# Feed-forward of a two-layer streaming encoder: the first three chunks' partial sums go into x by a ScalarE copy and an accumulating DMA

## The chip, the core and the metric

The kernel runs on one core of a Trainium2 chip. The engines named here are PE (TensorE, matrix products), DVE (VectorE), ACT (ScalarE), POOL (GpSimd) and SP (SyncE, which issues most loads); each serves its own queue strictly in order, and waits for other engines and for transfers by semaphores. TensorE writes its results into banks of PSUM; DVE and ACT read them there. The metric is the device time of one execution in microseconds (us), lower is better; a profiled execution also gives a span, from its first to its last instruction of the program.

## What is computed

A trunk of two layers over 512 tokens of width 1024, batch 1, in float32. Cut to what matters:

```python
def conv_ffn(xn, w_up, conv_w, conv_b, w_down):
    h = causal_depthwise_conv(xn @ w_up, conv_w) + conv_b
    g, u = jnp.split(h, 2, axis=-1)
    return (jax.nn.gelu(g) * u) @ w_down

for layer in range(2):
    x = x + mixer(rms_norm(x, mix_norm[layer]))
    x = x + memory_cross_attention(rms_norm(x, xattn_norm[layer]), ...)
    x = x + conv_ffn(rms_norm(x, ffn_norm[layer]), ...)
return rms_norm(x, final_norm)
```

The mixer is attention of two kinds in layer 0 and a gated recurrence (mLSTM) in layer 1. The feed-forward is the place of the change: the inner width is 2816, so `w_up` is 1024 x 5632 (a gate half and a value half) and `w_down` is 2816 x 1024.

## The kernel before

**Layout.** x is held transposed in SBUF for the whole run: eight tiles `x[m]` of 128 features x 512 tokens, float32. Every product is made of float32r operands split into a high and a low part, and `mm3` (lines 282 to 286) issues three matmuls for each: high x high, high x low, low x high. Weights come as blocks of 128 x 1024 (or 128 x 512) by SP into a raw tile (`raw`, `dr`, `sa`, `ra`); ACT casts the high part (`wh`), DVE subtracts it for the low part (`wl`).

**The feed-forward** is `ffn_steps` (from line 1155). The inner width is worked off as 22 pairs `p` of a gate block and a value block. Pairs 0 to 3 are `plain`: two up blocks of eight products. Pairs 4 to 21 are `seven`: a Strassen-like scheme with seven products of half-width operands (256 columns) in place of eight. It needs sums of weight blocks: `sa` is loaded by SP with one block and POOL then issues an accumulating DMA that adds the other block onto it (`onto`, line 1369; the only transfers on POOL's queue). DVE forms `sb` from `sa` and `raw`, and combines the products in the banks with a copy `v` that ACT makes (line 1428) and `u`, which DVE makes from it (line 1433) and on which further products wait. `tail` then runs the convolution (an ACT pass on line 1307, two DVE passes on line 1314, for each half), the GELU, the product of both halves and the split of the result into `ah` and `al`, the inputs of the down blocks.

**The down blocks.** The 22 pairs are grouped into five chunks, `CHUNKS` = four of four pairs and one of six. For chunk `c` and output tile `m` (0 to 7), `down(c, m)` loads a down block, issues 12 matmuls of 512 columns (4 pairs x 3) into one of the two banks `w`, and lets DVE add the bank to `x[m]` (`xadd`, line 523, the addition on line 526). Chunk 0's eight blocks are queued when pair 5 begins, chunk 1's at pair 9, chunk 2's at pair 13 and chunk 3's at pair 18; each pair takes two of them by `fill`, so that in the steady state a pair is seven narrow products and two down blocks. Five blocks of chunk 3 come after the last pair. Chunk 4 follows at the end of the feed-forward: in layer 0 as `down(4, m, 2)`, after each of which the norm of the next stage is prepared, in layer 1 in `finish`, with the final norm and the output.

**The order** is not that of the code. `Sched` (from line 143) is a list scheduler: each task names an engine, a duration, what it depends on, a priority (a due time), which buffers it takes and frees, and a latency. It plays all engines at once with those durations, lets each engine take whichever task can start first, and emits the instructions in that order. The banks `w`, and the raw tiles, are among the counted buffers. The order on each engine's queue is thus fixed ahead, by the planned times.

**The tile `sqt`** (128 x 512 float32, two buffers, in the pool `sp`) is a scratch tile: of the squares in `squares` (line 492), of the broadcasts in `bcast_cols` (line 450), of the gates of layer 1 and of `finish`.

Of the kernel before, what the change touches and what calls it, by code (L numbers as in the profile page):

```python
# [13 lines left out]
ALU = mybir.AluOpType  # L14
# [47 lines left out]
class Plan:  # L62
# [11 lines left out]
    def add(self, fn, dur=0.0, deps=(), prio=None, take=(), free=(), chain=(), pre=(), after=0.0, order=(), load=(), st=None):  # L74
        it = Item(fn, dur, [d for d in deps if d is not None], len(self.items) if prio is None else prio, take, free, chain, pre, after, order, load, st)
        it.n = len(self.items)
        self.items.append(it)
        return it
# [151 lines left out]
class Builder:  # L230
# [924 lines left out]
    def ffn_steps(self, layer, mp):  # L1155
# [1 line left out]


        nc, t = self.nc, self.t
        sc = Sched(raw=3, h=3, s2=1, s4=1, a22=1, sa=3, sb=2, ra=1, hs=2, c=1, dr=2, v=1, u2=1, u3=1, act=10, acc=4, s=2, w=2)  # L1160
        add = sc.add
        tt = lambda n: 0.055 + 1.06e-3 * n
        act = lambda n: 0.1 + 0.83e-3 * n
        ACV, STT = 0.71, 0.66
        clock = [0.0]
# [9 lines left out]
        def joined(deps, prio, free):  # L1175
            return add("-", 0.0, None, deps, prio, (), free, 0.0)
# [41 lines left out]
        def block(src, nk, xs, at, bank, deps, steps, tag="raw", off=0):  # L1218

            st, lo = weight(src, nk * P, at, tag, off)  # L1220
            last = None
            per = nk // steps
            for c in range(steps):

                def fn(c=c):
                    if c == 0:
                        st["ps"] = self.acc_bank(st["_acc"]) if bank == "acc" else self.bank(bank)
                    for k in range(c * per, (c + 1) * per):
                        self.mm3(st["ps"][:], *st["rows"](k), *xs(k), k == 0, k == nk - 1)

                last = pe(0.7 * per, fn, [lo, last, *deps], [(bank, st)] if c == 0 else (), [("h", st)] if c == steps - 1 else ())
            return st, last
# [35 lines left out]
        formed = []  # L1268
# [195 lines left out]
        xadded = [None] * 8  # L1464
        queue, late = [], []

        def down(c, m, steps=1):
            first, nk = CHUNKS[c]
            d, last = block(
                t[f"down{c}"][layer, m], nk, lambda k: tuple(a[:] for a in acts[first + k]), clock[0], "w", [acted[first + k] for k in range(nk)], steps,  # L1470
                "dr" if nk == 4 else "raw", OFF,
            )
            last.block, d["step"] = d, 16
            if m == 7:
                for k in range(nk):
                    joined([last], last.prio, [("act", acted[first + k].st)])
            e = add("DVE", 0.6, lambda: self.xadd(m, d["ps"]), [last, xadded[m], *formed], clock[0] + 3.0, (), [("w", d)])
            xadded[m] = e
            return e

        def fill():
            nonlocal queue
            if queue:
                down(*queue.pop(0))
# [15 lines left out]
        if layer == 0:  # L1500
            for m in range(8):
                e = down(4, m, 2)
                a = add("ACT", 1.2, lambda m=m: self.xprep(m, "mix", 1, state), [e], clock[0] + 3.0)
                add("DVE", 1.3, None, [a], clock[0] + 3.0)
# [370 lines left out]
```

## Time and profile before

| | |
|---|---|
| time, median of 3 runs | 1487.87 us (1487.7 to 1488.3) |
| the profiled execution: its time | 1488.21 us |
| the profiled execution: its span | 1486.4 us |
| granted TensorE clock | 0.999 |
| instructions | 22787 |
| bytes moved by DMA | 174.94 MB |
| feed-forward of layer 0, about | 419 to 740 us |
| feed-forward of layer 1, about | 1138 to 1486 us |

The profile shows, for each engine, the time in which it worked on an instruction (busy), the idle time ahead of an instruction and what ended it, and the chain of work that ended last, followed back from the last instruction. A row of a group reads: line, engine, operation, out<-in by the program's names, shapes, count | busy us in total, mean ns of one | idle us before them, by releaser. A row of the timeline reads: start us, duration us, engine, line, operation, names. DMA rows give the time from issue to landing. Rows of one engine can overlap, since the next instruction starts while the last one's results still drain.

### The profile page before, as it was taken

What the parts mean: (1) busy time and instruction counts of PE and PEld (TensorE: products, weight loads), DVE (VectorE), ACT (ScalarE), POOL (GpSimd) and SP (SyncE); (2) the same over time, 40 slices, a digit from 0 to 9 for tenths busy, and PEclk for the clock granted to TensorE, in tenths of its full rate; (3) what the DMA queues carried; (4) which work ended last, traced back from release to release, by engine and by line L of the source; (5) the groups of instructions that cost most, each with busy time, mean ns of one, the idle gap of its engine ahead of it and who ended that gap; (6) DMA issues with size and microseconds to landing.
All of it is one profiled execution on the core that took longest, in us unless ns stands there. A gap on an engine that the chain in (4) does not pass through costs nothing.

```text
span 1486.4 us, 22787 instructions
## 1 busy us (share of the span) xinstructions
PE 1474.2 (99%) x8570; PEld 1276.6 (86%) x8570; DVE 1207.3 (81%) x2332; ACT 814.7 (55%) x1372; POOL 61.6 (4%) x104
## 2 busy tenths in 40 slices
PE   9999999999999999999999999999999999999998
PEld 7888777888888999999888778888888899999987
DVE  7779795666679999999768857666567999999984
ACT  7777573444456555555446634444444655555554
POOL 0000130000001000000000000000000000000000
PEclk9999999999999999999999999999999999999999
DMA  5212223323237565662322222323323666656422
GB/s 196 86 63 79 86 79 121 122 78 128 72 131 201 163 150 168 157 157 77 92 96 86 71 99 77 108 85 119 123 71 121 169 171 157 171 154 160 117 67 78
DMA packets 62463, 174.94 MB, mean 118 GB/s; under 512 B 6800, under 2 KB 6800, under 8 KB 62352
## 3 DMA queue, kind: packets, MB, share of 16 engines
q1 hardware_dynamic: 56160, 153.48, 31.4%
q0 software_dynamic: 5184, 18.88, 7.5%
q8 instruction: 67, 1.10, 0.3%
q10 hardware_dynamic: 1008, 1.12, 0.2%
q14 instruction: 44, 0.36, 0.1%
HBM read 171.35 MB, written 2.10 MB: 117 GB/s over the span
## 4 chain that ended last, share of the span: by engine, by line
PE 81%; DVE 13%; ACT 2%; issue 2%; DMA 1%; ACTq 0%; DVEq 0%; SPq 0%
PE acc L284 16%; PE acc L285 16%; PE acc L286 16%; PE w L286 4%; PE w L284 4%; PE w L285 4%; DVE wl L275 3%; PE acc L345 3%; PE acc L347 2%; PE acc L346 2%; PE s L284 2%; PE s L285 2%; PE s L286 2%; DVE c L1314 2%; PE w L1660 1%
## 5 line engine op out<-in xcount | busy, mean ns | idle before, releaser
L284 PE MATMUL acc<-xh,wh 128*128 128x512 f32 (+1 forms) x800 | 284.2, 355 | 0.0
L286 PE MATMUL acc<-xh,wl 128*128 128x512 f32 (+1 forms) x800 | 279.6, 349 | 0.0
L285 PE MATMUL acc<-xl,wh 128*128 128x512 f32 (+1 forms) x800 | 279.4, 349 | 0.0
L275 DVE TENSOR_TENSOR wl<-raw,wh 128x1024 fp32r<-128x1024 f32 (+4 forms) x199 | 235.5, 1184 | 41.0 <-ACT wh L278 39.2
L278 ACT CAST wh<-raw 128x1024 fp32r<-128x1024 f32 (+1 forms) x135 | 139.4, 1035 | 162.7 <-PE acc L285 98.0
L286 PEld LDWEIGHTS acc<-xh,wl 128*128 128x128 f32 x800 | 150.2, 188 | 20.1
L285 PEld LDWEIGHTS acc<-xl,wh 128*128 128x128 f32 x800 | 150.4, 188 | 19.9
L284 PEld LDWEIGHTS acc<-xh,wh 128*128 128x128 f32 x800 | 150.3, 188 | 19.8
L1314 DVE SCALAR_TENSOR_TENSOR c<-hs,vec,c 128x512 f32<-128x512 f32 x176 | 129.5, 744 | 0.3
L286 PE MATMUL w<-ah,wl 128*128 128x512 f32 x304 | 119.0, 391 | 0.0
L284 PE MATMUL w<-ah,wh 128*128 128x512 f32 x304 | 118.7, 390 | 0.0
L285 PE MATMUL w<-al,wh 128*128 128x512 f32 x304 | 118.6, 390 | 0.0
L1307 ACT ACTIVATE c<-hs,vec 128x512 f32<-128x512 f32 x88 | 70.2, 813 | 46.9 <-DVE hs L1457 41.8
L1202 ACT CAST wh<-dr 128x512 fp32r<-128x512 f32 x64 | 39.5, 618 | 51.8 <-PE acc L285 16.7
L286 PEld LDWEIGHTS w<-ah,wl 128*128 128x128 f32 x304 | 57.1, 188 | 12.0
L284 PEld LDWEIGHTS w<-ah,wh 128*128 128x128 f32 x304 | 57.1, 188 | 10.5 <-ACT ah L1328 0.6
L285 PEld LDWEIGHTS w<-al,wh 128*128 128x128 f32 x304 | 57.1, 188 | 10.0
L284 PE MATMUL acc<-mem,wh 128*128 128x256 f32 (+1 forms) x192 | 61.5, 320 | 0.0
L286 PE MATMUL acc<-mem,wl 128*128 128x256 f32 (+1 forms) x192 | 61.0, 318 | 0.0
L285 PE MATMUL acc<-mem,wh 128*128 128x256 f32 (+1 forms) x192 | 60.8, 317 | 0.0
L526 DVE TENSOR_TENSOR x<-acc,x 128x512 f32<-128x512 f32 x32 | 22.1, 691 | 46.9 <-PE acc L286 46.9
L526 DVE TENSOR_TENSOR x<-w,x 128x512 f32<-128x512 f32 x72 | 49.2, 684 | 12.2 <-PE w L286 11.6
(390 smaller groups left out, 3950.7 us busy)
## 6 DMA issues: line engine op xcount, KB each, us to landing
raw<-in_up_dram SPq DMA_DIRECT2D x52, 512.0 KB, 3.4
sa<-in_up_dram SPq DMA_DIRECT2D x36, 512.0 KB, 4.3
sa<-in_up_dram POOLq DMA_DIRECT2D x36, 512.0 KB, 5.6
dr<-in_down_dram SPq DMA_DIRECT2D x64, 256.0 KB, 3.3
ra<-in_up_dram SPq DMA_DIRECT2D x36, 256.0 KB, 3.1
raw<-in_xk_dram SPq DMA_DIRECT2D x16, 512.0 KB, 3.3
raw<-in_wo_dram SPq DMA_DIRECT2D x16, 512.0 KB, 3.3
raw<-in_xq_dram SPq DMA_DIRECT2D x16, 512.0 KB, 3.3
```

Source lines behind the costliest of these rows:

```text
L275: self.nc.vector.tensor_tensor(out=lo, in0=v, in1=hi.bitcast(F32), op=ALU.subtract)
L278: self.nc.scalar.copy(hi, v)
L284: mm(out, wh, xh, start=first, stop=False, skip_group_check=parts)
L285: mm(out, wh, xl, start=False, stop=False, skip_group_check=parts)
L286: mm(out, wl, xh, start=False, stop=last, skip_group_check=parts)
L345: mm(ps, xh[k][:, ts], wh[:, ws], start=(k == 0), stop=False)
L346: mm(ps, xh[k][:, ts], wl[:, ws], start=False, stop=False)
L347: mm(ps, xl[k][:, ts], wh[:, ws], start=False, stop=(k == 7))
L526: self.nc.vector.tensor_tensor(out=self.x[m][:], in0=ps[:], in1=self.x[m][:], op=ALU.add)
L1202: nc.scalar.copy(st["wh"][:, :cols], st[tag][:, :cols])
L1307: nc.scalar.activation(st["c_"][:, j, :], hs()[:, j, 2:514], AF.Identity, scale=self.col("cw", (layer * 3 + 2) * 44 + blk), bias=self.col( ...
L1314: nc.vector.scalar_tensor_tensor(out=c, in0=hs()[:, j, n : n + 512], scalar=w, in1=c, op0=ALU.mult, op1=ALU.add)
```

## The change

For the chunks 0, 1 and 2 the DVE addition of `down` is replaced by two tasks: ACT copies the bank into a tile `sqt`, which gives the bank back, and POOL issues a DMA that accumulates `sqt` onto `x[m]`. The planner counts two buffers `sqt`, taken by the copy and given back when the DMA has landed (by its latency of 6.0). The wait for the earlier sum of the same `x[m]`, and for the sums of x that the seven-product scheme formed from it (`formed`), moves from the addition to the DMA. Chunks 3 and 4 stay as they were. There are 3 x 8 such sums in each of the two layers.

```diff
-        sc = Sched(raw=3, h=3, s2=1, s4=1, a22=1, sa=3, sb=2, ra=1, hs=2, c=1, dr=2, v=1, u2=1, u3=1, act=10, acc=4, s=2, w=2)
+        sc = Sched(raw=3, h=3, s2=1, s4=1, a22=1, sa=3, sb=2, ra=1, hs=2, c=1, dr=2, v=1, u2=1, u3=1, act=10, acc=4, s=2, w=2, sqt=2)
...
-            e = add("DVE", 0.6, lambda: self.xadd(m, d["ps"]), [last, xadded[m], *formed], clock[0] + 3.0, (), [("w", d)])
+            at = clock[0] + 3.0
+            deps = [xadded[m], *formed]
+            if c < 3:
+
+                def copied():
+                    d["sqt"] = self.til(self.sp, "sqt")
+                    nc.scalar.copy(d["sqt"][:], d["ps"][:])
+
+                def onto():
+                    nc.gpsimd.dma_start(self.x[m][:], d["sqt"][:], accum_op=ALU.add)
+
+                a = add("ACT", act(512), copied, [last], at, [("sqt", d)], [("w", d)])
+                e = add("POOL", 1.5, onto, [a, *deps], at + 1.0, (), (), 6.0)
+                joined([e], at, [("sqt", d)])
+            else:
+                e = add("DVE", 0.6, lambda: self.xadd(m, d["ps"]), [last, *deps], at, (), [("w", d)])
             xadded[m] = e
             return e
```

## The prediction

> **What bounds the kernel now.** I read the page first: the totals, the slices, and the chain of work that ended last.
>
> ```profile
> span 1486.4 us, 22787 instructions
> PE 1474.2 (99%) x8570; PEld 1276.6 (86%) x8570; DVE 1207.3 (81%) x2332; ACT 814.7 (55%) x1372; POOL 61.6 (4%) x104
> ...
> PE   9999999999999999999999999999999999999998
> ...
> DVE  7779795666679999999768857666567999999984
> ...
> PE 81%; DVE 13%; ACT 2%; issue 2%; DMA 1%; ACTq 0%; DVEq 0%; SPq 0%
> ```
>
> TensorE is busy throughout; VectorE is full only in slices 13 to 19 and 32 to 38, which are the two feed-forwards. The chain runs through DVE for 13% of the span, so it could be DVE that sets the end there. That decides the case, so I asked for the stretches in which the 24 changed sums of a layer stand (480 to 654 us, and the same in layer 1 some 719 us later).
>
> ```profile
> L526 DVE TENSOR_TENSOR x<-w,x x24: 676/684/692, 480.4 to 653.0; 128x512 f32<-128x512 f32 x24
> ...
> core 0: us, PE busy (x) PEld busy (x) DVE busy (x) ACT busy (x) POOL busy (x), PEclk, DMA share, GB/s
> 475.00:656.00 181.00, 181.00 (x1295) 168.53 (x1294) 179.38 (x305) 100.80 (x158) 11.13 (x13) 1.00 0.60 158
> 1194.00:1375.00 181.00, 180.88 (x1295) 168.44 (x1294) 179.38 (x306) 100.83 (x159) 11.15 (x13) 1.00 0.60 159
> ...
> 541.00:656.00 115.00, 115.00 (x827) 107.46 (x826) 113.39 (x192) 63.27 (x100) 6.84 (x8) 1.00 0.60 161
> ```
>
> Both engines are at 99 to 100% and the clock is full. A busy PE may still hide short stalls, since its rows overlap and their ends are modelled, so I measured its pace from starts in the timeline.
>
> ```profile
> 571.94 0.28 PE L284 MATMUL s<-xh,s4h 128*128 128x256 f32 x1
> 573.20 0.28 PE L286 MATMUL s<-xh,s4l 128*128 128x256 f32 x1
> 574.68 0.39 PE L284 MATMUL w<-ah,wh 128*128 128x512 f32 x1
> 577.18 0.40 PE L286 MATMUL w<-ah,wl 128*128 128x512 f32 x1
> 589.72 0.39 PE L284 MATMUL w<-ah,wh 128*128 128x512 f32 x1
> ```
>
> A block of twelve products spans eleven starts: (573.20 - 571.94)/11 = 0.1145 us for 256 columns, (577.18 - 574.68)/11 = 0.2273 us for 512. One pair of blocks has seven products of twelve narrow matmuls and two down blocks of twelve wide ones: 84 x 0.1145 + 24 x 0.2273 = 15.07 us. The pair really recurs after 589.72 - 574.68 = 15.04 us. So TensorE streams without a gap; DVE, at almost the same load, only keeps up with it. **TensorE is the bound, and the change touches none of its instructions.**
>
> How much could come free is what PE still waits for DVE in the two feed-forwards:
>
> ```profile
> L284 PE MATMUL acc<-th,wh 128*128 128x256 f32 x144 | 40.0, 278 | 0.4 <-DVE u L1433 0.4
> ...
> 705.10 0.38 PE L284 MATMUL acc<-th,wh 128*128 128x256 f32 x1 [0.18 <-DVE u L1433]
> ```
>
> This wait occurs once in each layer, some 50 us after the last changed sum. With the overlap of rows (0.28 - 0.11 = 0.16 us) each is 0.34 us long: 0.7 us. Inside the stretches PE lacks 0.12 us of 1194:1375, 0.3 us with the overlap. All that can be gained is about 1.0 us.
>
> **The change, part by part.** It removes 48 DVE sums (3 chunks x 8 rows of x x 2 layers).
>
> ```profile
> L526 DVE TENSOR_TENSOR x<-w,x 128x512 f32<-128x512 f32 x72 | 49.2, 684 | 12.2 <-PE w L286 11.6
> ...
> 572.36 0.68 DVE L526 TENSOR_TENSOR x<-w,x 128x512 f32<-128x512 f32 x1
> 573.03 1.23 DVE L275 TENSOR_TENSOR wl<-sa,wh 128x1024 fp32r<-128x1024 f32 x1
> ...
> 577.78 0.68 DVE L526 TENSOR_TENSOR x<-w,x 128x512 f32<-128x512 f32 x1
> 578.38 0.74 DVE L1314 SCALAR_TENSOR_TENSOR c<-hs,vec,c 128x512 f32<-128x512 f32 x1
> 587.18 0.69 DVE L526 TENSOR_TENSOR x<-w,x 128x512 f32<-128x512 f32 x1 [0.19 <-PE w L286]
> 592.82 0.68 DVE L526 TENSOR_TENSOR x<-w,x 128x512 f32<-128x512 f32 x1
> ```
>
> A row is 0.684 us, but the next starts 0.60 us after it (577.78 to 578.38), so each sum frees 0.60 us: 48 x 0.60 = 28.8 us of DVE, 1.2 us in each 15.04 us pair. All of it lies beside PE's unbroken stream. On the path it is worth 0 to 1.0 us; I take 0.6, because the 705 us wait has chunk 3's sums, which stay on DVE, still ahead of it.
>
> It adds 48 ScalarE copies out of the bank. The nearest row is the same shape elsewhere:
>
> ```profile
> L1662 ACT COPY num<-w 128x512 f32<-128x512 f32 x8 | 4.7, 582 | 7.2 <-PE w L1660 7.2
> ...
> L1384 ACT CAST wh<-sa 128x1024 fp32r<-128x1024 f32 x36 | 37.8, 1051 | 28.7 <-PE w L285 18.8 <-PE acc L285 4.3 <-issue 4.2
> ```
>
> 24 x 0.582 = 14.0 us on ACT's 100.8 of 181: 63%. The bank is now given back by ACT. The block that starts at 574.68 ends at 577.58, and its bank is wanted again by the block of 589.72; DVE gave it back at 578.46. ACT's copy, even behind its longest cast (1.05 us), gives it back by 579.5: ten microseconds of cover, price 0. If that cover were gone, every microsecond would be PE's.
>
> The copy is a wait on PE's last matmul in ACT's queue. Behind it stand the convolution passes and the copy `v`, on which DVE's `u` and then a product wait:
>
> ```profile
> 577.35 0.82 ACT L1307 ACTIVATE c<-hs,vec 128x512 f32<-128x512 f32 x1 [1.97 <-DVE hs L1457]
> ...
> 578.59 0.82 ACT L1307 ACTIVATE c<-hs,vec 128x512 f32<-128x512 f32 x1
> 579.31 0.36 ACT L1428 ACTIVATE v<-acc 128x256 f32<-128x256 f32 x1
> ...
> 581.04 0.42 DVE L1433 TENSOR_TENSOR u<-acc,v 128x256 f32<-128x256 f32 x1
> ```
>
> `v` ends at 579.67 and `u` starts at 581.04: 1.37 us of slack against 0.58 us of copy. Price between 0 and what the second rival below works out; I take 0, since ACT idles 45% and waits (1.97 us) just ahead.
>
> It adds 48 accumulating transfers of 256 KB on POOL's queue, which so far carries only the accumulating loads of `sa`:
>
> ```profile
> L1370 POOL DMA_DIRECT2D sa<-in_up_dram x36: 847/860/999, 448.3 to 1384.6; - x36
> ...
> DMA to landing us min/median/max: 5.1/5.6/10.3
> ...
> 578.33 0.86 POOL L1370 DMA_DIRECT2D sa<-in_up_dram  x1 [13.19 <-DVE sb L1390]
> ...
> 590.48 0.68 DVE L1390 TENSOR_TENSOR sb<-sa,raw 128x512 f32<-128x512 f32 x1
> ...
> q1 hardware_dynamic: 6749, 14.61, 39.5%
> q0 software_dynamic: 1036, 3.76, 20.0%
> ...
> sa<-in_up_dram POOLq DMA_DIRECT2D x8, 512.0 KB, 6.4
> dr<-in_down_dram SPq DMA_DIRECT2D x15, 256.0 KB, 2.8
> ```
>
> POOL: 48 x 0.86 = 41 us, in a queue that idles 13 us out of 15. An `sa` load issued at 578.33 lands 6.4 us later, at 584.7, and its first reader starts at 590.48: 5.8 us of slack, against 2 x 0.86 us if both of a pair's new issues go first. Price 0. Landing of the new transfer: no row shows it; between the 2.8 us of a plain 256 KB load and the 10.3 us of the worst accumulate; I take 5, nearer the median accumulate. The scratch tile `sqt` has two buffers, so a buffer is reused after two blocks, 577.78 to 592.82 = 15.0 us: copy, issue and even 10.3 us make 11.7, so ACT does not wait for a buffer (its other users, the squares and the broadcasts of the norms, run outside these stretches). Chunk 3's sum of the same row of x, on DVE, comes eight blocks (60 us) later. Price 0. SP's queue is not passed by anything.
>
> Transfer time, over 541:656 (16 new transfers, 4.19 MB): by bytes of the accumulating queue 20.0% x 4.19/3.76 = 22%, by its packets (1036 over 3.76 MB make 144 for a load of 128 rows, and x has 128 rows too) 20.0% x 2304/1036 = 44%. The share goes from 60% to 82 or 104%. I take the bytes, since a plain transfer of half the size also lands sooner; the price is 0 below 100%.
>
> **Sum.** -0.6 + 0 + 0 + 0 us. The profiled execution took 1488.21 us (span 1486.4 and 1.8 around it), 0.3 above the median of the runs; from it the sum gives 1487.6, from the median 1487.87 it gives **1487.3 us**.
>
> **A rule against the change.** POOL's issue rows are 847 to 999 ns while DVE is 98.6% busy (113.39 of 115). The Trainium skill (SBUF — State Buffer, "SBUF: two separate sides") warns that POOL cannot write the descriptors of its transfers while VectorE runs an operation that takes both ports, and gives 620 ns growing to about 3100 ns. By that, an estimate from the page, each issue would be 2.5 us longer and three of them in a pair would use up the slack of `sa`; by the rows there is no such growth, so the trace does not agree for this kernel's two-input operations.
>
> **The rivals.**
> 1. *DVE was the bound after all* (for: the chain's 13%; against: 15.07 computed and 15.04 seen). Each pair then shrinks by 1.2 us, 24 pairs: 1487.9 - 28.8 = 1459 us. Chance 5%.
> 2. *Slower: ACT's queue becomes the wait.* If the planner puts the copy ahead of the first convolution pass of 577.35, that pass starts after the block's end plus the copy (577.58 + 0.2 + 0.58 = 578.4), 1.05 us late; with the pair's other copy (0.58) `v` is 1.6 us late. It decides from 1.37 us. The excess of 0.27 us is PE's, 24 times: 6.5 us, 1494.4. For: ACT is served strictly in order; against: the freed DVE does its part of the same loop earlier. Chance 13%.
> 3. *Slower: the transfers fill the DMA engines.* If a 2 KB row costs as much as a 4 KB one, the share is 104% and the two stretches stretch by 4.5% of 362 us: 16 us, 1504. It decides from 100%. Chance 9%.
> 4. *Slower: descriptors are written only in DVE's gaps* (the rule above). A pair has (115 - 113.39)/115 x 15.04 = 0.2 us of gap, 1.4 after the change; three issues need 2.6. Short by 1.2 us, 24 times: 28 us, 1516. Against: today 0.86 fits no gap of 0.2, and is not longer for it. Chance 1%.
>
> **How the numbers follow.** Forecast 72%; it alone spans 1486 to 1489 (gain up to 1.0, and runs 0.6 us apart). The range 1485.5 to 1495 adds the second rival and leaves out 15%. A measurement can tell about 0.2% (3 us) from no change: within that 72% (the forecast), faster 5% (first rival), slower 23% (the three others).
>
> **What will show it.** Right: in 475:656 PE stays at 181 of 181, DVE falls by 24 x 0.60 to about 165, ACT rises to about 115, POOL to 32, the DMA share to about 0.8; 24 sums of `w` into x stay in L526; POOL rows stay near 0.86 us. The pair still recurs after 15.04 us. Wrong: pairs that recur later, with PE waiting for `u` (ACT's queue), for `sb` through `sa` (POOL or DMA), or for a `w` bank; or a pair shorter than 15.0 us, which would mean that PE's pace was not its own.

## The result and the profile after

The changed kernel takes 1490.12 us (median of 22 runs, 1489.43 to 1490.64) against 1488.14 for the kernel before (22 runs, 1487.70 to 1488.74): 1.98 us more, a ratio of 1.0013 with a 95% interval from 1.0007 to 1.0019. A second series of both kernels, each beside 33 runs of the kernel before, gave 1489.81 and 1488.19, 1.62 us apart. That is less than the 0.2% (3 us) that the prediction took as the bound of "no change", and inside its range of 1485.5 to 1495.0; but it is more than the runs scatter, and it goes the other way than the 0.6 us gain that was forecast.

First the page of the changed kernel: totals, two rows of slices, the accumulating queue and the chain of waits.

```profile
span 1487.8 us, 22952 instructions
PE 1473.8 (99%) x8570; PEld 1276.5 (86%) x8570; DVE 1184.8 (80%) x2284; ACT 832.6 (56%) x1420; POOL 103.3 (7%) x152
...
DVE  7779795666689999999768857666566999999984
...
POOL 0000130000001111110000000000000011111000
...
q0 software_dynamic: 12096, 31.46, 12.1%
...
PE 84%; DVE 11%; ACT 2%; issue 2%; DMA 0%; SPq 0%; ACTq 0%; DVEq 0%
```

Next the same stretches as before the change (columns: stretch, length, busy time of PE, PEld, DVE, ACT and POOL, granted clock, DMA share, GB/s).

```profile
475.00:656.00 181.00, 180.20 (x1290) 167.81 (x1289) 167.67 (x280) 109.65 (x182) 30.90 (x37) 1.00 0.79 191
1194.00:1375.00 181.00, 180.43 (x1291) 168.04 (x1290) 167.72 (x281) 109.68 (x182) 30.23 (x35) 1.00 0.80 192
541.00:656.00 115.00, 115.00 (x826) 107.45 (x825) 104.42 (x173) 68.72 (x115) 19.72 (x24) 1.00 0.80 194
```

The change does what it says: 24 fewer sums on DVE, 24 more copies on ACT, POOL and the DMA engines busier, near the predicted sizes but for ACT, which rose by 8.9 us in place of 14. From 541 us on PE is still unbroken. What PE lost, 0.80 and 0.57 us of the two long stretches, lies ahead of that. The rows of the new copies and transfers (duration in ns, min/median/max):

```profile
L1483 ACT COPY sqt<-w x48: 566/578/588, 480.5 to 1373.5; 128x512 f32<-128x512 f32 x48
L1486 POOL DMA_DIRECT2D x<-sqt x48: 843/860/1211, 481.4 to 1376.2; - x48
```

The issues are of two kinds: 28 took 0.84 to 0.87 us, and 20 took 1.05 to 1.21 us, each of these starting 0.5 to 0.7 us after an `sa` issue, whose row of 0.86 us it overlaps. The transfers land after 6.2 us in the median (3.3 to 8.2). So I looked for PE's gaps. Two of the four are these, in the timeline of the changed kernel, PE first and DVE after it:

```profile
511.12 0.28 PE L285 MATMUL acc<-tl,a22h 128*128 128x256 f32 x1
511.69 0.38 PE L284 MATMUL s<-xh,s4h 128*128 128x256 f32 x1 [0.29 <-DVE hs L1433]
...
526.03 0.40 PE L286 MATMUL w<-ah,wl 128*128 128x512 f32 x1
526.93 0.39 PE L284 MATMUL s<-xh,s4h 128*128 128x256 f32 x1 [0.51 <-DVE hs L1433]
```

```profile
509.15 0.41 DVE L1433 TENSOR_TENSOR u<-acc,v 128x256 f32<-128x256 f32 x1
509.49 1.21 DVE L275 TENSOR_TENSOR wl<-raw,wh 128x1024 fp32r<-128x1024 f32 x1
510.62 0.68 DVE L275 TENSOR_TENSOR al<-c,ah 128x512 fp32r<-128x512 f32 x1
511.22 0.41 DVE L1433 TENSOR_TENSOR hs<-u,s 128x256 f32<-128x256 f32 x1
...
525.00 0.42 DVE L1433 TENSOR_TENSOR u<-acc,v 128x256 f32<-128x256 f32 x1
525.33 1.22 DVE L275 TENSOR_TENSOR wl<-raw,wh 128x1024 fp32r<-128x1024 f32 x1
526.47 0.42 DVE L1433 TENSOR_TENSOR hs<-u,s 128x256 f32<-128x256 f32 x1
```

`hs<-u,s` (the task `c22` of `seven`, which turns one product's bank into a part of `hs`) needs only `u` and a bank that is long done, and PE's next narrow product overwrites that bank, so it waits for `hs`. In the changed kernel DVE subtracts a whole weight block for the next pair, 1.2 us, between the two. In the kernel before, at the first of the two places, DVE and then PE:

```profile
510.15 0.42 DVE L1433 TENSOR_TENSOR u<-acc,v 128x256 f32<-128x256 f32 x1
510.48 0.68 DVE L1324 TENSOR_TENSOR c<-c 128x512 f32<-128x512 f32 x1
511.08 0.41 DVE L1433 TENSOR_TENSOR hs<-u,s 128x256 f32<-128x256 f32 x1
```

```profile
511.26 0.28 PE L285 MATMUL acc<-tl,a22h 128*128 128x256 f32 x1
511.55 0.39 PE L284 MATMUL s<-xh,s4h 128*128 128x256 f32 x1
```

PE waits for `hs` there too, but less: 0.29 us from start to start, where its pace is 0.11, against 0.57 in the changed kernel. No `wl<-raw` stands between `u` and `hs` in any pair of the kernel before (where anything does, it is shorter, as `c<-c` here); the change brings it into two pairs of each layer. Nothing in those two instructions was edited. The planner's list for the changed kernel has `hs` right behind `u` in every pair; the queue that runs is laid out once more from it, so its order is not fixed by the planned times alone, as I wrote of the kernel before, and there the two differ. A likely reason is that the low part of the weight is ready earlier once DVE has lost its sums; that, and the rule by which it then goes ahead, no run here shows. What experiments 1 and 8 show is that leaving the sums out of the plan is enough to bring it about, and counting them in it undoes it.

To add up, I cut each trace at the first product `s<-xh,s4h` of pair 4 (472.64 us before, 472.27 after) and at the start of the last matmul (1479.81 and 1480.36):

| us, two profiles each | before | after |
|---|---|---|
| start to the cut in pair 4 | 472.64, 472.83 | 472.27, 472.48 |
| from there to the last matmul | 1007.17, 1007.03 | 1008.09, 1008.05 |
| last matmul to the end of the span | 6.60, 6.59 | 7.44, 7.42 |
| around the span | 1.80, 1.77 | 2.09, 1.95 |

The loss of 0.9 to 1.0 us between the cuts lies in the feed-forwards: from the first `s<-xh,s4h` of the last pair of layer 0 to that of pair 4 of layer 1 both kernels take 481.49 us. The end, whose code was not touched, lost 0.83 us, and 0.2 to 0.3 more stand around the span. The two losses had to be explained apart.

### The profile page after: what moved, and what is told of

Same layout as the page of the kernel before. It is cut to its first block, busy times and chain, and to the rows that moved or that the text cites. A ratio compares the mean times of both kernels' runs of the same rounds, so it can differ in the third digit from the quotient of the medians.

```text
span 1487.8 us, 22952 instructions
## 1 busy us (share of the span) xinstructions
PE 1473.8 (99%) x8570; PEld 1276.5 (86%) x8570; DVE 1184.8 (80%) x2284; ACT 832.6 (56%) x1420; POOL 103.3 (7%) x152
## 3 DMA queue, kind: packets, MB, share of 16 engines
q0 software_dynamic: 12096, 31.46, 12.1%
## 4 chain that ended last, share of the span: by engine, by line
PE 84%; DVE 11%; ACT 2%; issue 2%; DMA 0%; SPq 0%; ACTq 0%; DVEq 0%
PE acc L284 17%; PE acc L285 17%; PE acc L286 17%; PE w L284 4%; PE w L286 4%; PE w L285 4%; PE acc L345 3%; PE acc L346 3%; PE acc L347 3%; DVE wl L275 2%; PE s L284 2%; PE s L285 2%; PE s L286 2%; DVE c L1314 2%; PE w L1675 1%
## 5 line engine op out<-in xcount | busy, mean ns | idle before, releaser
L286 PEld LDWEIGHTS w<-ah,wl 128*128 128x128 f32 x304 | 57.1, 188 | 12.1
L1486 POOL DMA_DIRECT2D x<-sqt x48 | 47.4, 988 | 155.7 <-ACT sqt L1483 155.7
L1384 ACT CAST wh<-sa 128x1024 fp32r<-128x1024 f32 x36 | 37.8, 1050 | 34.2 <-issue 26.1
```

The source lines that it names most:

```text
L286: mm(out, wl, xh, start=False, stop=last, skip_group_check=parts)
L1384: nc.scalar.copy(s["wh"][:, :cols], raw())
L1486: nc.gpsimd.dma_start(self.x[m][:], d["sqt"][:], accum_op=ALU.add)
```

## The experiments

Theory A says that the order on DVE's queue costs the time; theory B, that the copies, the transfers or POOL's issues do. Times are medians of 11 runs, differences are against the kernel before in the same series; "main part" is the time from the cut in pair 4 to the last matmul, 1007.1 us before and 1008.1 after.

**1. No sums at all.**

```diff
             if c < 3:
+                joined([last], at, [("w", d)])
+                return last
```

> Leaves out the sums of chunks 0 to 2 altogether (neither VectorE's addition, nor the copy, nor the transfer), so x lacks these parts. VectorE's queue then has the changed kernel's order: twice a layer a weight's low part `wl<-raw` (1.2 us) stands between `u` and `hs<-u,s`. Theory A (the order on VectorE's queue costs the time): the waits of the product `s<-xh,s4h` for `hs<-u,s` at about 511, 526, 1230 and 1245 us are there as after the change (0.3 to 0.7 us each), and the time is 0.9 to 2.0 us over the kernel before, 1489.0 to 1490.1. Theory B (the copies on ScalarE, the transfers or POOL's issues cost it, wherever): none of them is left, so the time is at or below the kernel before, 1487.5 to 1488.2.

1489.26 us, +1.08 (ratio 1.0008, 0.9999 to 1.0017), main part 1008.22. PE waits as in the changed kernel, on the same queue order:

```profile
511.92 0.28 PE L285 MATMUL acc<-tl,a22h 128*128 128x256 f32 x1
512.52 0.39 PE L284 MATMUL s<-xh,s4h 128*128 128x256 f32 x1 [0.32 <-DVE hs L1433]
```

DVE and PE run the same instructions in the same order as in the changed kernel. Work was taken away and put nowhere, and the main part is 1.1 us longer. Theory B falls for the main part.

**2. The sum held ahead.** The changed kernel; the next pair's weight subtraction (the task marked `behind`) is put on DVE's queue behind the last `hs<-u,s` (`owner.ahead`).

```diff
+            if getattr(t, "behind", False) and owner.ahead is not None:
+                with owner.tc.issue_after(owner.ahead):
+                    t.fn()
```

> The changed kernel, with `hs<-u,s` held ahead of the next pair's weight subtraction `wl<-raw` on VectorE's queue; copies and transfers as in the change. Theory A: the four waits at 511, 526, 1230 and 1245 us go back to what they were before the change (0.17 us or less, 0.28 in layer 1), and the time falls by at least 0.9 us against the changed kernel, to 1488.1 to 1489.2; if all of the loss is the order, to 1488.1. Theory B: nothing changes, 1490.1.

1487.23 us, -0.95 (ratio 0.9993, 0.9983 to 1.0002), main part 1005.49. The second place, in this kernel:

```profile
525.94 0.40 PE L290 MATMUL w<-ah,wl 128*128 128x512 f32 x1
526.18 0.28 PE L288 MATMUL s<-xh,s4h 128*128 128x256 f32 x1
```

The four waits are gone, and more: it is 2.6 us shorter than the changed kernel in the main part, and 1.6 us shorter than the kernel before. Theory A had allowed for the 0.9 us alone. The edit moved little else: besides the four `hs`, in each layer one `sb<-sa,raw` on DVE, one convolution pass on ACT and five `a22h` or `a22l` matmuls on PE were moved. The pairs 6 to 9, from one `s<-xh,s4h` to another, took 556.90 - 495.88 = 61.02 us before, 557.13 - 495.49 = 61.64 after, and 556.26 - 495.99 = 60.27 here:

```profile
495.99 0.30 PE L288 MATMUL s<-xh,s4h 128*128 128x256 f32 x1
...
556.26 0.28 PE L288 MATMUL s<-xh,s4h 128*128 128x256 f32 x1
```

The first and the last row of the same in the kernel before, and in the changed one:

```profile
495.88 0.39 PE L284 MATMUL s<-xh,s4h 128*128 128x256 f32 x1
...
556.90 0.28 PE L284 MATMUL s<-xh,s4h 128*128 128x256 f32 x1
```

```profile
495.49 0.30 PE L284 MATMUL s<-xh,s4h 128*128 128x256 f32 x1
...
557.13 0.28 PE L284 MATMUL s<-xh,s4h 128*128 128x256 f32 x1
```

So PE already lost 0.75 us here before the change, in waits of 0.1 to 0.2 us that hardly show as idle time; the busy time of 181.00 of 181 had hidden them. In layer 1 the same four pairs took 60.97 us before, 61.46 after, and 60.17 here.

**3 and 4. Parts of the change.** `if c in (1, 2)` and `if c == 0` in place of `if c < 3`.

> Chunk 0's sums stay on VectorE; chunks 1 and 2 go by copy and transfer: two thirds of the copies and transfers. On VectorE's queue the first pairs have the order of the kernel before; one `wl<-raw` a layer, two pairs later than in the changed kernel, still stands ahead of `hs<-u,s`. Theory A: one wait a layer instead of two, 0.3 to 0.7 us each, 0.5 to 1.0 us over the kernel before: 1488.6 to 1489.1. Theory B: two thirds of 2.0 us, +1.3: 1489.4.

> Only chunk 0's sums go by copy and transfer: one third of them. VectorE's queue has the changed kernel's order at the same two pairs of each layer. Theory A: the same four waits, and the changed kernel's time or at least its 0.9 us: 1489.0 to 1490.1. Theory B: one third of 2.0 us, +0.7: 1488.8.

Chunks 1 and 2: 1489.81 us, +1.63 (1.0011, 1.0002 to 1.0019), main part 1008.16. Chunk 0 alone: 1489.25, +1.07 (1.0007, 0.9998 to 1.0016), main part 1007.83. The first was dearer than theory A said: its one new wait a layer is 0.27 us (at 556.95 and 1276.08), but it keeps the small waits of the kernel before as well, and the pairs behind gain nothing. The second puts a third of the copies in and has 0.7 of the 1.0 us in the main part. Theory B's proportions (1.3 and 0.7) don't fit the two either, and the times alone would not have told the theories apart; the places of the waits did.

**5 to 7. What copies and transfers cost by themselves**, on the kernel with the sum held ahead: without both, with the copies only, and with each transfer issued as two.

```diff
-                    nc.gpsimd.dma_start(self.x[m][:], d["sqt"][:], accum_op=ALU.add)
+                    for o in (0, 256):
+                        nc.gpsimd.dma_start(self.x[m][:, o : o + 256], d["sqt"][:, o : o + 256], accum_op=ALU.add)
```

> The kernel with `hs<-u,s` held ahead, and the sums of chunks 0 to 2 left out altogether (no addition, no copy, no transfer: x lacks these parts). From the first product of pair 4 to the last matmul it should take what the kernel with the sum held ahead took, 1005.5 us. Theory C (beyond the order, each transfer or copy costs some 0.015 us outside TensorE's stream, 0.7 us for 48): 0.7 us less than with them, 1486.5. Theory D (the rest is scatter between kernels): 1487.2.

> The kernel with `hs<-u,s` held ahead and ScalarE's 48 copies, but without the 48 transfers (x lacks the parts of chunks 0 to 2). Theory C1 (the rest lies in the transfers and POOL's issues): 1486.5, as without both. Theory C2 (it lies in ScalarE's copies): 1487.2, as with both.

> The kernel with `hs<-u,s` held ahead, each of the 48 transfers issued as two of half the columns: 96 issues on POOL, the same bytes in twice the rows. Theory C1 with a price per issue or per row: twice the 0.7 us, 1487.9. With a price per byte, or theory D: 1487.2. If the transfers filled the DMA engines (my third rival: twice the rows makes them hold more of the engines' time), pairs would recur later than 15.04 us and the time would rise by 10 us or more.

Without both 1486.63 us (-1.33), copies only 1487.04 (-0.92), two halves 1486.58 (-1.38; ratio 0.9990, 0.9982 to 0.9999). Twice the issues and rows cost nothing: theory C1 falls, and the main parts (1005.51, 1005.34 and 1005.72 us) leave 0.4 us at most for all of it. The first of them, beside experiment 1 (1008.22 us), is also the cleanest pair for theory A: no sums, copies or transfers in either, and 2.7 us between them for the place of `hs` and the few moves that came with it. The page of the kernel with halves, the accumulating queue, and the window of 541:656 in it:

```profile
q0 software_dynamic: 19008, 31.47, 12.9%
```

```profile
541.00:656.00 115.00, 115.00 (x831) 107.60 (x830) 104.57 (x174) 69.72 (x116) 32.24 (x38) 1.00 0.84 193
```

6912 packets more raise the queue's share from 12.1 (12.0 in experiment 2) to 12.9% and the DMA share from 0.80 to 0.84. The queue had 7.5% before the change, so the new transfers' own share went from 4.6 to 5.4% when their rows were doubled: it went mostly by the bytes.

**8. The planned order kept**, by an entry of 0.6 us on DVE that the planner counts and nobody issues.

```diff
                 joined([e], at, [("sqt", d)])
+                add("DVE", 0.6, None, [last, *deps], at)
```

> The changed kernel, with the planner still counting an addition of 0.6 us on VectorE that is not issued: the planned order is that of before, the work that of the change. On VectorE's queue no `wl<-raw` then stands between `u` and `hs<-u,s`; from the second of these pairs on it is the shorter `wl<-dr`, of half a block. Theory A: the waits of 0.5 and 0.7 us at 511 and 526 us are gone (0.2 us at most each), and the time lies 0.9 us or more below the changed kernel: 1488.3 to 1489.2. Theory B: 1490.1.

1487.61 us, -0.35 (0.9997, 0.9988 to 1.0006), main part 1005.89. Below the expected 1488.3: a short `wl<-dr` (0.28 us) stands ahead of `hs`, and PE waits no longer for it. The rest of DVE's order is not that of experiment 2. This second way to keep `wl<-raw` behind `hs` gains 2.2 us on the changed kernel in the main part, where experiment 2 gained 2.6.

**9 and 10. How late `hs` may be.** In the kernel with the sum held ahead, eight pairs of each layer write `hs<-u,s` three or five times.

```diff
-                self.ahead = tt_(out=hs(1, 1)(), in0=tmp("u3")(), in1=bank("R")(), op=ALU.subtract).ins
+                for _ in range(3 if 9 <= p < 17 else 1):
+                    self.ahead = tt_(out=hs(1, 1)(), in0=tmp("u3")(), in1=bank("R")(), op=ALU.subtract).ins
```

> The kernel with `hs<-u,s` held ahead; in eight pairs of each layer (9 to 16) this sum is written three times over with the same values, so that it ends 2 x 0.33 = 0.66 us later. In the kernel with the sum held ahead it ends 0.80 us before the product that reads it starts, and never less than 0.05 us before in any pair: 0.75 us of lateness are free. Theory A: no wait, the pair still recurs after 15.04 us, 1486.6 to 1487.2 us. Rival (DVE's busy time counts, wherever it lies): 16 x 0.66 = 10.6 us more, 1497.5.

> The same with the sum written five times over: it ends 4 x 0.33 = 1.32 us later, 0.57 us more than the 0.75 us that are free. Theory A: TensorE waits 0.57 us for `hs` in each of 16 pairs, 15.6 us from pair to pair, 9.1 us over the kernel with the sum held ahead: 1496. Rival (VectorE still has idle time in each pair, so nothing is lost): 1486.6 to 1487.2.

Three times: 1490.04 us, 2.8 over experiment 2, where 0 was expected. Five times: 1491.23, 4.0 over it, where 9 was expected. The first miss is a size, as the three sums show on DVE, and the pairs from the first to the last row on PE:

```profile
570.29 1.33 DVE L1453 TENSOR_TENSOR hs<-u,s 128x256 f32<-128x256 f32 x3
```

```profile
541.34 0.38 PE L288 MATMUL s<-xh,s4h 128*128 128x256 f32 x1
...
647.67 0.33 PE L288 MATMUL s<-xh,s4h 128*128 128x256 f32 x1
```

The repeated sums follow each other after (1.33 - 0.42)/2 = 0.455 us, not 0.33. `hs` is thus 0.91 us late, 0.16 over the 0.75 us that are free: 16 x 0.16 = 2.6 us. The seven pairs between the two rows take 106.33 us, 15.19 each in place of 15.04. In that very stretch PE's busy time is 106.33 of 106.33 us:

```profile
541.34:647.67 106.33, 106.33 (x757) 98.03 (x757) 101.70 (x176) 63.51 (x105) 18.16 (x21) 1.00 0.79 191
```

DVE is busy for 101.70 us of it, less than the 98.6% it had before the change, and yet PE waits for it. The Trainium skill (Trainium Kernel Development and Optimization, "Performance Expectations") calls the busy time of matmuls a bad measure of how close a kernel is to roofline (its limit), because they are pipelined; here the trace agrees, with 1 us lost in a stretch that is 100% busy. With five sums, `hs` is 1.83 us late, and the queue of PE in the trace is another: matmuls with `a22h`, which need not wait for `hs`, now stand ahead of `s4h` (nine of them from 572.02 us on) and cover most of it.

**11 and 12. Both kernels again.**

> The kernel before, unchanged: what two series of the same kernel differ by, and a second profile of its start and its end (472.6 us up to the first product of pair 4; 6.6 us from the last matmul's start to the end of the span; 1.8 us around the span). Theory C (the rest of the loss lies in the end, which is the kernel's own): 6.6 and 1.8 again. Theory D (it scatters): they differ by some tenths, 6.6 to 7.4 and 1.8 to 2.1.

> The changed kernel, unchanged: a second profile. From the first product of pair 4 to the last matmul 1008.1 us again (1007.2 before the change). Theory C: 7.4 us from the last matmul's start to the end of the span and 2.1 around it again, 1.1 us more than before. Theory D: as the other kernels, 6.9 to 7.2 and 1.8 to 2.0, and the remaining loss of the time stands in no one place.

1488.19 us (1.0001, 0.9992 to 1.0010) and 1489.81 (1.0011, 1.0002 to 1.0020); their cuts stand in the table above. The end repeats within 0.02 us for each kernel and is 0.83 us longer in the changed one. So it is no scatter, and it doesn't go with the number of transfers: with the sum held ahead it is 6.96 us with 48 transfers, 6.94 with 96 and with none, and 7.19 with the copies alone (experiment 6); without that edit it is 6.96 with 16 transfers and with none, 7.13 with 32 (experiment 3), and with 48 it is 7.43 in the change but 6.95 in experiment 8. What does differ is instruction loading. The stretch from 1480.3 us to the end holds, by DMA queue, after the change:

```profile
q10 hardware_dynamic: 561, 1.02, 28.5%
q1 hardware_dynamic: 470, 0.83, 23.0%
q14 instruction: 3, 0.02, 0.7%
```

Before the change there is no row of an instruction queue at that place. In the changed kernel the first of the three 8 KB fetches starts at 1482.05 us, among the output's transfers, and the output's last one lands 5.94 us after the last matmul's start, not 5.46; the second starts at 1487.58 behind SyncE's last waits, one of which begins 0.37 us after its predecessor in place of 0.06. The two other kernels whose end is above 7 us have a fetch among the output's transfers too (3.16 us after the last matmul's start in experiment 3, 1.33 in experiment 6), and none of those so far with an end of 6.96 us or less has one. The third fetch starts after the span. What stands around the span goes with it, in all twenty profiles of this document: 1.77 to 1.80 us in the eight profiles without a fetch there, 1.89 to 2.11 in eleven of the twelve with one (experiment 5 is the exception, 1.78).

**13 to 16. Moving the instruction counts.** Theory L: where an engine's fetch falls depends on how many instructions it has run, so a count that is moved moves the fetch. VectorE gets 24 fills of one element at the start, SyncE 12 transfers of four bytes in the first feed-forward, or both; the fourth is SyncE's in the kernel with the sum held ahead.

```diff
+        for i in range(24):
+            nc.vector.memset(self.spare[:1, i % 4 : i % 4 + 1], 0.0)
...
+                if (layer, p) == (0, 12):
+                    with self.tc.issue_after(i):
+                        for k in range(12):
+                            nc.sync.dma_start(self.spare[:1, 4 + k : 5 + k], acts[p - 2][0][:1, k : k + 1].bitcast(F32))
```

> The changed kernel with 24 fills of one element on VectorE at the very start, so that its instruction count at the end is 24 higher. Theory L (the loading of instructions at the end costs the rest: VectorE's block of 8 KB is fetched among the output's transfers): the fetch at 1.7 us after the last matmul's start is gone, the last output lands 5.46 us after it in place of 5.94, the end comes at 6.95 in place of 7.43, the time falls by 0.5 to 1489.4. SyncE's pause of 0.37 us in its last waits stays. Rival (the transfers or another part of the change delay the output): the end stays at 7.43, the time at 1489.8 to 1490.1.

> The changed kernel with 12 transfers of four bytes more on SyncE's queue, in the middle of the first feed-forward, so that its instruction count at the end is at least 12 higher. Theory L: the pause of 0.37 us between two of SyncE's last waits is gone (0.06 us as between the others) and the fetch behind it; the outputs still land at 5.94; the end comes at 7.05 in place of 7.43. Rival: the pause stays. If the first feed-forward is longer than 237.8 us, the added transfers hold SyncE's queue and the time is judged by the end alone.

> The changed kernel with both additions. Theory L: the end at 6.6 us as in the kernel before, and 0.8 to 1.05 us less than the changed kernel: 1488.9 to 1489.2, which leaves the 0.9 us of TensorE's waits. Rival: 1489.8 to 1490.1.

> The kernel with `hs<-u,s` held ahead and the 12 small transfers on SyncE. Theory L: its end goes from 6.96 to 6.6 us, the time from 1486.6-1487.2 to 1486.2-1486.9, 1.4 to 1.7 us below the kernel before. Rival: 6.96 stays.

| | start to cut | main part | end | around | median us |
|---|---|---|---|---|---|
| changed, again | 472.48 | 1008.05 | 7.42 | 1.95 | 1489.81 |
| VectorE +24 | 473.24 | 1007.87 | 6.64 | 2.02 | 1489.95 |
| SyncE +12 | 472.83 | 1007.88 | 6.82 | 2.11 | 1489.60 |
| both | 472.90 | 1007.93 | 6.33 | 1.79 | 1489.66 |
| sum ahead, SyncE +12 | 472.88 | 1005.63 | 6.35 | 2.05 | 1486.66 |

In the traces theory L holds. With VectorE's count moved, the fetch among the outputs is gone and the last output lands at 5.46 us again; SyncE's long pause went with it, which I had not expected (SyncE has one instruction more there). With SyncE's count moved, the fetch among the outputs stays at 1.7 us and the pause is gone. With both, no instruction is fetched in the whole end, and it is shorter than in the kernel before. The times follow only in part (against 1489.81, from another series): 0.15 us for both, against the 0.8 to 1.05 expected, 0.2 for SyncE, none for VectorE. The start is 0.35 to 0.76 us longer in these profiles than in the changed kernel's, VectorE's fills stand in it in two of them, and it scatters from 472.3 to 473.5 us over all kernels. That the fetches lengthen the end is shown; that they are the whole rest of 1 us in the time is not. Nor does any row say which engine a fetch is for: that is inferred from which count moves it.

**17 and 18. Does the gain need the change?** The kernel before with the sum held ahead (`if c < 3` made `if False`), beside the changed one with it.

> The kernel before, all sums on VectorE, with `hs<-u,s` held ahead of the next `wl<-raw`. Theory A1 (the gain needs the time that the change frees): in the kernel before no `wl<-raw` stands ahead of `hs` anyway, and with VectorE at 99% `hs` cannot come earlier; 1007.1 us from the first product of pair 4 to the last matmul, 1488.1 as the kernel before. Theory A2 (holding the sum ahead is the whole gain): 1005.5 us there and 1486.6 to 1487.2.

> The changed kernel with the sum held ahead, again: 1005.5 us from the first product of pair 4 to the last matmul, an end of 6.96 us, 1486.8 to 1487.3.

1487.99 us (0.9999, 0.9990 to 1.0008), main part 1007.01; and 1486.82 (0.9992, 0.9983 to 1.0001), main part 1005.48. The second run repeats the gain. The first is no test of theory A1, since `wl<-raw` stands behind `hs` in the kernel before anyway: the edit moved nothing, DVE, PE, POOL and SyncE run the same instructions in the same order, and this is the kernel before once more. So this fix is worth something only beside the change. That DVE must first have the time is argued, not shown: holding `hs` ahead of the shorter `c<-c` and `al<-c`, which stand before it in the kernel before, was not tried. The changed kernel with the sum held ahead, in its forms of experiments 2, 7, 16 and 18, takes 1486.58 to 1487.23 us: 0.95 to 1.49 below the kernel before, and some 3 below the change as it stands. It is the best version found; for two of the four (halves, and 12 transfers on SyncE) the interval of the ratio ends below 1.

## Why the prediction failed

**"All of it lies beside PE's unbroken stream. On the path it is worth 0 to 1.0 us; I take 0.6."** This is the step that failed, at both ends. I counted the freed 28.8 us of DVE as time that can only help and kept every other instruction where it was. But the queue's order is made from the work that is in it: with the sums gone, a 1.2 us subtraction came to stand ahead of the sum that PE waits for, twice a layer, and the main part lost 1.0 us where 0.6 was to be gained (experiments 1 and 2). The upper end was also too low: with the order mended, the same freed time is worth 1.6 us, since PE lost more than the 1.0 us that I found as idle time: 1.55 us in pairs 6 to 9 of the two layers, by starts (experiment 2).

**PE is the bound; the pair recurs after 15.04 us.** Right from pair 10 on: 587.21 - 572.17 = 15.04 us, PE 115.00 of 115.

```profile
572.17 0.28 PE L284 MATMUL s<-xh,s4h 128*128 128x256 f32 x1
...
587.21 0.28 PE L284 MATMUL s<-xh,s4h 128*128 128x256 f32 x1
```

It was wrong for the four pairs ahead of it (6 to 9), where the fill of down blocks is still shifting; my check of the pace was taken in one place, at 572 to 590 us.

**Sizes.** DVE's busy time in 475:656 fell to 167.67 us, where 165 was predicted: 0.49 us a sum, not 0.60. ACT's copy took 0.578 us (0.582 predicted), but ACT's busy time rose to 109.65 us only (115 predicted), 0.37 us a copy, since rows overlap. POOL's issue stayed at 860 ns in the median and its stretch came to 30.90 us (32 predicted). The rule of the Trainium skill (SBUF — State Buffer, "SBUF: two separate sides") by which POOL would wait for VectorE with its descriptors is again not borne out: the longest of 48 issues took 1211 ns, behind another issue, with VectorE busy for 93% of the stretch. But the Trainium skill states it there for operations in a 2-port perf mode, and no row here shows in which mode an operation ran: the runs clear this kernel and do not refute the rule. The landing was 6.2 us (5 taken) and the DMA share 0.79 to 0.80 (0.82 by bytes, 1.04 by rows); experiment 7 bears out the choice of bytes.

**The rivals.** That DVE was the bound (1459 us) falls with experiment 1: without the sums PE is no faster. ACT's queue (1494.4): the copies are in experiment 2, which is faster than the kernel before. DMA engines filled (1504): experiment 7 doubles the rows at no cost. Descriptors (1516): the rows above. The loss came from none of them.

**The signs.** "PE with 181 of 181" failed by 0.80 and 0.57 us, and pointed at the place. Of the wrong signs I listed `u`, `sb` and a bank; the one that came was `hs`, off the engine that had been relieved.

**The end.** I gave it no term, since nothing there was edited. It cost 0.83 us in the span and 0.2 to 0.3 around it in both profiles, and goes with the loading of instructions (experiments 11 to 16).

## What to carry to other kernels

Work taken off a nearly full engine also changes the order of what is left on it. Before costing it at "nothing or a gain", list the short instructions on it that the bounding engine waits for, and see what long and ready instruction could now be put ahead of each; then fix that order. And measure the pace of the bounding engine over every pair of the loop, by starts, since a busy time of 100% hid 0.15 us in each pair here.

## What the runs showed of the hardware

Instructions are fetched by DMA while the kernel runs (in the changed kernel 45 transfers of 8 KB on queue q14 and 67 of 16 KB on q8), and a fetch among the last output transfers made the last of them land 0.5 us later (5.94 against 5.46 us). The same subtraction of VectorE, written again to the same place, starts 0.455 us after the one before it (experiment 9), where the next instruction into another tile follows after 0.33 (510.10 to 510.43 us in experiment 2). An accumulating transfer of 256 KB from SBUF to SBUF landed after 6.2 us in the median, hardly sooner in two halves of 128 KB (5.9 us).
